# Softmax attention output made turned, with split operands and gates scaled and turned beforehand: one change to a two-layer hybrid decoder kernel

## The chip, the cores and the metric

The kernel runs on one core of one Trainium2 chip. The metric is the device time in microseconds of one execution. Five queues of instructions run side by side on the core and wait for each other by semaphores: TensorE (PE, with its weight loads as PEld), VectorE (DVE), ScalarE (ACT), GpSimd (POOL) and SyncE (SP), which here issues nearly all DMAs.

## The reference

Two layers over 256 positions of 1024 values. In each layer one input projection gives eight groups of 512 columns: query, key, value and gate of four retention heads (rq, rk, rv, rz) and of four softmax attention heads (mq, mk, mv, mz). With 256 positions there is a single block, so the block selection chooses nothing and the softmax attention is plain causal attention with a bias.

```python
for i in range(DEPTH):
    h = rms_norm(x, norm_g[i])
    rq, rk, rv, rz, mq, mk, mv, mz = jnp.split(h @ w_in[i], cuts, axis=-1)
    r_out = retention(rotary(rq), rotary(rk), rv, ret_norm_g[i])   # decayed scores, per-head norm
    r_out = silu(rz) * r_out
    m_out = moba(rms_norm(mq, q_norm_g[i]), rms_norm(mk, k_norm_g[i]), mv, rel_bias)
    m_out = silu(mz) * m_out                                       # softmax(q k + bias) v, gated
    x = x + concatenate([r_out, m_out], -1) @ w_out[i]
    gate = sigmoid(rms_norm(x) @ w_ple_gate[i])
    x = x + gate * rms_norm(p[i] @ w_ple[i], ple_norm_g[i])
```

## The kernel before

**Arithmetic.** Weights and activations are f32. A projection is made of three fast matmuls of 512 columns (lines 405 to 407): each operand is split into a high part, rounded to the fast type f32r, and a low part, the rest, and high x high, high x low and low x high are summed. A split is a cast on ScalarE and a subtraction on VectorE: `Stage.gen` does it for two rows of weights at a time (cast L350, subtraction L353). `three` is the same for an attention product. A few small products (L950, L960, L1010) are plain f32 matmuls instead.

**Layout.** Positions are cut into two halves `m` of 128. A projection's result has positions on the partitions. What must be turned goes through `halves` (a ScalarE copy that parts the 16-bit halves into a tile `u16`, L621), a turning DMA from SP's queue into `w16` (L631), and two VectorE copies per turned tile (L640); `to_parts` then splits it into high and low for a projection, as the tile `yT` (called `a` in the profile).

**Order within a layer.** Input projections in the order mq, mk, rq, rk, mz, mv, rv, rz; after the first ones, at places that `groups` names, the attention products: `moba_scores` (softmax scores, then `probs`: bias, exponential, turning into the tile PT, named PS in the profile); `moba_out` (the softmax product by `pv`, L960, followed at once by the retention scores of the last 128 positions, L1010); `ret_scores` (L932); `ret_out` (the retention product, L960 again). The retention scores are multiplied by the decay on VectorE (`decayed`, L999) before `ret_out` may read them. Then come the output projection (k-rows 4 to 7, the softmax half, first), the embedding product and the gate.

**What sets the order.** TensorE's order is that in which the program is written. The other engines' instructions come from chains (generators) that ask a planner, `Flow`, for an engine, a cost, and what must be there or be free; the planner keeps a clock for each engine and lays the ready instruction with the earliest due time. The planned costs decide only the order: on the chip each engine takes its instructions strictly in that order. `tick` starts a group of products when what it needs is done by the planner's clock, with a margin:

```python
groups.append(([lambda: [PC.get(k) for k in ((0, 0), (1, 0), (1, 2))], both(VC, MV), both(TC, RQ, RK)],
               moba_out, 3, 2.0))
groups.append(([], ret_scores, 2, 2.2))
groups.append(([lambda: [SC.get(h) for h in ("own", 0, 2)], both(VC, RV)], ret_out, 2, 0.3))
```

The last number is the margin in microseconds; the one before is the number of free banks wanted of the four of the accumulator pool `mix`.

**Around the softmax product.** `value` makes V on ScalarE (L868). `gate` makes silu's tanh part, kept in G. `moba_y` takes the product from its bank: for each of four heads one VectorE operation with the reciprocal of the softmax sum and the gate (L978), then `halves` and `to_parts` into `yT`.

## Time and profile before

| what | value |
|---|---|
| median of 3 runs | 296.58 us (296.27 to 297.05) |
| profiled execution: span | 294.1 us |
| profiled execution: own whole time | not on the page; the median lies 2.5 us above the span |
| PE busy | 288.9 us, 98% of the span, 1411 instructions |
| PEld / DVE / ACT / POOL busy | 246.5 / 253.5 / 214.7 / 30.9 us |
| softmax and retention output products (L960), both layers | 96 records, 11.4 us |
| retention and softmax scores in three terms (L932) | 48 records, 6.3 us |

How to read it: the page describes one execution. A plain f32 matmul leaves two records, a fast one leaves one. Matmuls overlap in the pipeline, so the mean duration of a group is longer than the distance between starts; the distance is what a matmul costs in a dense stream, and the same holds on VectorE by some 0.09 us an instruction.

### The profile page before, as it was taken

The page shows a single profiled execution, that of the slowest core. Times are in us where ns is not written, and L with a number is a line of the kernel's source. Part 1 is how long each engine was busy: PE and PEld are TensorE (multiplying, and loading weights), DVE is VectorE, ACT ScalarE, POOL GpSimd, SP SyncE. Part 2 cuts the span into 40 slices and gives each one's busy share as a digit, 9 for nine tenths or more (in the row PEclk, how much of TensorE's full clock was granted, in tenths as well). Part 3 has the DMA queues.
Part 4 walks back from the last instruction along what each step waited for, and adds up shares of the span by engine and source line. Part 5 has one row for each costly group of instructions (what it writes and reads, how often), then busy time and mean ns, then how long its engine had stood idle before and what let it go on. Part 6 is the DMA issues. An engine that isn't in the chain of part 4 may idle for free.

```text
span 294.1 us, 4301 instructions
## 1 busy us (share of the span) xinstructions
PE 288.9 (98%) x1411; PEld 246.5 (84%) x1411; DVE 253.5 (86%) x461; ACT 214.7 (73%) x376; POOL 30.9 (11%) x44
## 2 busy tenths in 40 slices
PE   8999999999999999999999999999999999999994
PEld 4788888888899888888888888888898988888884
DVE  3967799999899999699999589999998797969942
ACT  3979974799747893998585896599646869479411
POOL 5004200000001200022003220000000030001300
PEclk9999999999999999999999999999999999999999
DMA  7999999998969868698689969787999766943021
GB/s 220 378 403 410 290 244 309 377 290 187 245 193 270 337 150 280 152 245 319 166 198 296 370 187 220 281 222 170 242 322 243 274 226 176 295 89 71 0 75 71
DMA packets 61774, 69.77 MB, mean 237 GB/s; under 512 B 46260, under 2 KB 47160, under 8 KB 61624
## 3 DMA queue, kind: packets, MB, share of 16 engines
q1 hardware_dynamic: 61712, 69.50, 79.7%
q8 instruction: 11, 0.18, 0.3%
q14 instruction: 11, 0.09, 0.1%
q0 software_dynamic: 32, 0.01, 0.0%
q10 hardware_dynamic: 8, 0.00, 0.0%
HBM read 57.42 MB, written 1.05 MB: 199 GB/s over the span
## 4 chain that ended last, share of the span: by engine, by line
PE 96%; DMA 2%; SPq 0%; ACT 0%; DVE 0%; issue 0%
PE acc L406 26%; PE acc L405 26%; PE acc L407 26%; PE acc L553 4%; PE mix L960 4%; PE mix L932 2%; DMA a<-in_early 2%; PE mix L407 1%; PE mix L743 1%; PE mix L742 1%; PE mix L406 1%; PE mix L744 1%; PE mix L405 1%; PE mix L1010 1%; PE mix L950 1%; ACT wh L459 0%
## 5 line engine op out<-in xcount | busy, mean ns | idle before, releaser
L405 PE MATMUL acc<-wh,a 128*128 128x512 f32 (+1 forms) x286 | 107.8, 377 | 0.0
L406 PE MATMUL acc<-wl,a 128*128 128x512 f32 (+1 forms) x286 | 107.7, 377 | 0.0
L407 PE MATMUL acc<-wh,a 128*128 128x512 f32 (+1 forms) x286 | 107.4, 376 | 0.0
L353 DVE TENSOR_TENSOR wl<-wst,wh 128x1024 fp32r<-128x1024 f32 x76 | 92.0, 1222 | 9.1 <-ACT wh L350 8.9
L350 ACT CAST wh<-wst 128x1024 fp32r<-128x1024 f32 x76 | 78.6, 1054 | 15.2 <-PE acc L407 6.0
L405 PEld LDWEIGHTS acc<-wh,a 128*128 128x128 f32 x286 | 53.5, 187 | 9.1
L407 PEld LDWEIGHTS acc<-wh,a 128*128 128x128 f32 x286 | 53.5, 187 | 9.0
L406 PEld LDWEIGHTS acc<-wl,a 128*128 128x128 f32 x286 | 53.5, 187 | 8.7
L621 ACT COPY u<-tok 128x1024 uint16<-128x1024 uint16 x30 | 31.1, 1053 | 12.7 <-DVE tok L978 7.9
L657 ACT CAST a<-tmp 128x512 fp32r<-128x512 f32 x20 | 12.4, 618 | 10.9 <-DVE tmp L654 8.3
L621 ACT COPY u<-x_t 128x1024 uint16<-128x1024 uint16 x12 | 12.5, 1042 | 10.2 <-DVE x_t L1138 6.8
L673 POOL TENSOR_TENSOR ro<-rs_t,neghalf 128x4 f32<-128x4 f32 x4 | 5.8, 1460 | 129.0 <-DVE rs_t L671 129.0
L640 DVE COPY tmp<-w 128x512 uint16<-128x512 uint16 x40 | 16.4, 466 | 0.1
L659 DVE TENSOR_TENSOR a<-tmp,a 128x512 fp32r<-128x512 f32 x20 | 13.7, 685 | 0.0
L640 DVE COPY T<-w 128x512 uint16<-128x512 uint16 x32 | 12.9, 467 | 0.7 <-DMA w<-u 0.7
L553 PE MATMUL acc<-wh,a 128*128 128x512 f32 (+1 forms) x42 | 11.3, 387 | 0.3 <-ACT wh L459 0.3
L960 PEld LDWEIGHTS mix<-V,PS 128*128 128x128 f32 x96 | 11.3, 192 | 0.3
L1189 DVE SCALAR_TENSOR_TENSOR tmp<-tmp,E 128x512 f32<-128x512 f32 (+1 forms) x9 | 5.7, 629 | 6.7 <-ACT tmp L1183 3.8
L960 PE MATMUL mix<-V,PS 128*128 128x128 f32 x96 | 11.4, 275 | 0.0
L1186 ACT ACTIVATE tmp<-acc,hr 128x512 f32<-128x512 f32 (+1 forms) x8 | 5.0, 631 | 8.5 <-PE acc L407 8.5
L405 PE MATMUL acc<-T,a 128*128 128x512 f32 (+1 forms) x30 | 11.0, 367 | 0.0
L407 PE MATMUL acc<-T,a 128*128 128x512 f32 (+1 forms) x30 | 10.9, 365 | 0.0
(144 smaller groups left out, 458.2 us busy)
## 6 DMA issues: line engine op xcount, KB each, us to landing
wst<-in_w_in SPq DMA_DIRECT2D x59, 512.0 KB, 6.3
wst<-in_w_out SPq DMA_DIRECT2D x16, 512.0 KB, 6.6
wst<-in_w_gate SPq DMA_DIRECT2D x16, 512.0 KB, 4.6
wst<-in_w_ple SPq DMA_DIRECT2D x4, 512.0 KB, 7.6
wst<-in_early SPq DMA_DIRECT2D x4, 384.0 KB, 7.4
a<-in_early SPq DMA_DIRECT2D x3, 384.0 KB, 5.8
x_t<-in_x SPq DMA_DIRECT2D x1, 1024.0 KB
gb<-in_ple_g SPq DMA_DIRECT2D x2, 512.0 KB, 6.7
```

The source lines that it names most:

```text
L350: nc.scalar.copy(hi, s)
L353: nc.vector.tensor_tensor(lo, s, hi.bitcast(F32), op=ALU.subtract)
L405: nc.tensor.matmul(ps, ah, wh, start=start, stop=False)
L406: nc.tensor.matmul(ps, ah, wl, start=False, stop=False)
L407: nc.tensor.matmul(ps, al, wh, start=False, stop=stop)
L553: nc.tensor.matmul(ps[m][:, sl], (a0.lo if which[0] == "lo" else a0.hi)[:, k, m * P:(m + 1) * P], columns(w, sl), start=start and i + j == ...
L621: nc.scalar.copy(u, src.bitcast(U16).rearrange("p (n t) -> p t n", t=2))
L640: nc.vector.tensor_copy(v, w[:, t].rearrange("p (h b) k -> p h (b k)", h=v.shape[1]))
L657: nc.scalar.copy(h, src)
L659: nc.vector.tensor_tensor(a.lo[:, k0:k0 + 4, m * P:(m + 1) * P], src, h.bitcast(F32), op=ALU.subtract)
L932: nc.tensor.matmul(ps, w[a], x[b], start=i == 0, stop=i == 2)
L960: nc.tensor.matmul(ps[:, h * DH:(h + 1) * DH], lhs(h, m, b), v[:, b, h * DH:(h + 1) * DH], start=b == 0, stop=b == m)
```

## The change

The softmax product is made turned: V is the stationary operand, and the probabilities move, so the product comes out with head dimension on the partitions and positions along the row, as the output projection wants it. For the first block of 128 keys, which all 256 positions see, it is made in three fast rows of 256 columns a head, from split operands; for the second block, which only the last 128 positions see, it stays one plain f32 matmul of 128 columns a head. For this `value` splits the first half of V into high and low (`box["VT"]`), and `probs` splits the first key block of the probabilities, both into places of `yT` that are not yet used. The gate is multiplied by the reciprocal of the softmax sum and turned ahead of the product (`gate_turned`), by `halves`, a turning DMA and copies into PT; `moba_y` then needs one multiplication by the turned gate and the split, two heads at a time, and no turning. The tile for the decayed retention scores, which shares its buffer with PT, is taken in `decayed` and no longer on TensorE's side.

```diff
         def value(g, m, ps):
...
+            if m or g == RV:
+                nc.scalar.activation(V[g][:, m], ps, AF.Copy, scale=scale)
+            else:
+                hi, lo = box["VT"] = [yT.both[:, k].rearrange("p t s -> p (t s)") for k in (6, 7)]
+                nc.scalar.activation(hi, ps, AF.Copy, scale=scale)
+                yield ask(DVE, 0.665)
+                nc.vector.scalar_tensor_tensor(lo, ps, scale, hi.bitcast(F32), op0=ALU.mult, op1=ALU.subtract)
...
             yield from turned(u, lambda: raw[:, :, h0:h0 + per, m * P:m * P + n])
+            src, hi, lo = (v[:, h0:h0 + per, m * P:(m + 1) * P] for v in (box["PT"], yT.hi, yT.lo))
+            yield ask(ACT, 0.1 + 0.11 * per)
+            nc.scalar.copy(hi, src)
+            yield ask(DVE, 0.08 + 0.13 * per)
+            nc.vector.tensor_tensor(lo, src, hi.bitcast(F32), op=ALU.subtract)
...
+        def turn_gates():
+            for m in range(MT):
+                if (MZ, m) in GC and (m, 2 * m) in PC and m not in GTC:
+                    GTC[m] = flow.begin(gate_turned(m), flow.soon(GATES))
+
+        def gate_turned(m):
             ri = small(H, "ri")
-            yield ask(DVE, 0.1)
+            yield ask(DVE, 0.1, after=(GC[MZ, m], *PC.values()))
             nc.vector.reciprocal(ri, DEN[m])
             yield ask(DVE, 0.14)
             nc.vector.tensor_scalar(ri, ri, stats(m)[1], None, op0=ALU.mult)
-            yield ask(DVE, 0.26, take=("tok",), after=(GC[MZ, m],))
...
-                nc.vector.scalar_tensor_tensor(y[:, sl], ps[:, sl], ri[:, h:h + 1], G[MZ][:, m, sl],
-                                               op0=ALU.mult, op1=ALU.mult)
+            yield ask(DVE, 0.605, take=("tok",))
+            o = tok_p.tile([P, GW], F32, name="tok")
+            nc.vector.tensor_tensor(o.rearrange("p (h d) -> p h d", h=H), G[MZ][:, m].rearrange("p (h d) -> p h d", h=H),
+                                    ri[:, :, None].to_broadcast([P, H, DH]), op=ALU.mult)
...
-            u = yield from halves(y, "tok")
-            yield from to_parts(yT, m, 4, u)
+            u = yield from halves(o, "tok")
+            raw = box["PT"].bitcast(U16).rearrange("p h (k t) -> p t h k", t=2)
+            yield from turned(u, lambda: raw[:, :, :, m * P:(m + 1) * P])
+
+        def moba_y(i, ps):
+            yield ask(DVE, 0.605, take=("tmp",), after=tuple(GTC[m] for m in range(MT)))
+            t = tmp_p.tile([P, GW], F32, name="tmp").rearrange("p (h s) -> p h s", h=2)
+            nc.vector.tensor_tensor(t, ps.rearrange("p (h s) -> p h s", h=2), box["PT"][:, i::2, :S], op=ALU.mult)
+            flow.free("mix")
...
+            yield ask(ACT, 0.53)
+            hi, lo = (v[:, H + i::2] for v in (yT.hi, yT.lo))
+            nc.scalar.copy(hi, t)
+            yield ask(DVE, 0.605)
+            nc.vector.tensor_tensor(lo, t, hi.bitcast(F32), op=ALU.subtract)
...
         def moba_out():
-            for m in range(MT):
-                ps = pv(m, lambda h, m, b: box["PT"][:, h, (m + b) * P:(m + b + 1) * P], V[MV])
...
+                for h, d, o in heads:
+                    flow.row(0.342)
+                    three(o, [v[:, d] for v in (vh, vl)], [v[:, h] for v in (yT.hi, yT.lo)], False)
+                for h, d, o in heads:
+                    flow.row(0.22)
+                    nc.tensor.matmul(o[:, P:], V[MV][:, 1, d], box["PT"][:, h, S:], start=False, stop=True)
...
         def decayed(h0, n, cols, ps):
-            yield ask(DVE, 0.605, after=(L_DEC,))
+            own = n == H
+            yield ask(DVE, 0.605, take=("PS",) if own else (), after=(L_DEC,) if own else (L_DEC, SC["own"]))
```

**What the planner makes of it.** Line numbers of helpers move by one (the weight split's subtraction L353 is L354 after, the copies L640 are L641). Names carry buffer numbers here.

TensorE in layer 0, at the softmax product and the own-block scores. Before:

```order
L960 MATMUL mix_971<-V_901,PS_662 128x128 x4
L960 MATMUL mix_980<-V_901,PS_662 128x128 x8
L1010 MATMUL mix_1001<-T_762,T_865 128x128 x4
L405 MATMUL acc_900<-wh_887,a_132 128x512
L406 MATMUL acc_900<-wl_888,a_132 128x512
```

After (L949 is `three`, L1034 the plain matmul of the second key block):

```order
L949 MATMUL mix_1023<-a_139 128x256 x3
L949 MATMUL mix_1024<-a_139 128x256 x3
L1034 MATMUL mix_1023<-PS_662,V_917 128x128
L1034 MATMUL mix_1024<-PS_662,V_917 128x128
L949 MATMUL mix_1023<-a_139 128x256 x3
L949 MATMUL mix_1024<-a_139 128x256 x3
L1034 MATMUL mix_1023<-PS_662,V_917 128x128
L1034 MATMUL mix_1024<-PS_662,V_917 128x128
L1060 MATMUL mix_1048<-T_762,T_867 128x128 x4
```

The product moved behind 18 more projection rows (from the middle of rv's 48 into the first rows of rz); between the own-block scores and `ret_scores` stand twelve rows where six stood, and between `ret_scores` and `ret_out` six where eighteen stood. In layer 1 the product moved behind 30 more rows, with twelve rows in each of the two places.

VectorE in layer 0, from the last copies of probabilities to the softmax product's own operations. Before:

```order
L640 COPY PS_662<-w16_885 128x2x256 x2
L353 TENSOR_TENSOR wl_910<-wst_691,wh_909 128x1024
L767 TENSOR_TENSOR pl_790<-pf_787,ph_789 128x512
L353 TENSOR_TENSOR wl_932<-wst_744,wh_931 128x1024
L640 COPY T_865<-w16_922 128x4x128 x2
L353 TENSOR_TENSOR wl_953<-wst_848,wh_952 128x1024
L969 RECIPROCAL ri_979<-den_663 128x4
L971 TENSOR_SCALAR ri_979<-ri_979,hr_376 128x4
L978 SCALAR_TENSOR_TENSOR tok_987<-mix_971,ri_979,G_810 128x128 x4
L353 TENSOR_TENSOR wl_973<-wst_903,wh_972 128x1024
```

After, the first part (L878 is V's split, L945 the probabilities', L1001 the gate's scaling):

```order
L641 COPY PS_662<-w16_888 128x2x256 x2
L878 SCALAR_TENSOR_TENSOR a_139<-acc_793,rstd_375,a_139 128x512
L945 TENSOR_TENSOR a_139<-PS_662,a_139 128x2x128 x2
L354 TENSOR_TENSOR wl_911<-wst_691,wh_910 128x1024
L996 RECIPROCAL ri_778<-den_663 128x4
L998 TENSOR_SCALAR ri_778<-ri_778,hr_376 128x4
L1001 TENSOR_TENSOR tok_957<-G_812,ri_778 128x512
L996 RECIPROCAL ri_788<-den_664 128x4
L998 TENSOR_SCALAR ri_788<-ri_788,hr_401 128x4
L1001 TENSOR_TENSOR tok_969<-G_812,ri_788 128x512
L814 TENSOR_TENSOR Q2_925<-T_867,Q2_925 128x512
L354 TENSOR_TENSOR wl_938<-wst_744,wh_937 128x1024
```

V's split, two splits of probabilities and the gates' scaling, with its reciprocals, now stand ahead of the product; before, the reciprocals stood behind it.

VectorE in layer 0, where the softmax product's result and the retention decays are taken from their banks (the third part of the same list). Before:

```order
L978 SCALAR_TENSOR_TENSOR tok_1015<-mix_980,ri_999,G_810 128x128 x4
L999 TENSOR_TENSOR PS_1000<-mix_1001,cst_122 128x4x128
L999 TENSOR_TENSOR PS_1000<-mix_1021,cst_122 128x2x256
L999 TENSOR_TENSOR PS_1000<-mix_1033,cst_122 128x2x256
L640 COPY tmp_1051<-w16_1013 128x512 x2
```

After (L1013 is the multiplication by the turned gates, L1021 the split of its result, L1051 the decays):

```order
L354 TENSOR_TENSOR wl_993<-wst_903,wh_992 128x1024
L641 COPY PS_662<-w16_986 128x4x128 x2
L768 TENSOR_TENSOR pl_792<-pf_789,ph_791 128x512
L641 COPY PS_662<-w16_1000 128x4x128 x2
L354 TENSOR_TENSOR wl_1011<-wst_959,wh_1010 128x1024
L1013 TENSOR_TENSOR tmp_1054<-mix_1023,PS_662 128x512
L1013 TENSOR_TENSOR tmp_1060<-mix_1024,PS_662 128x512
L1051 TENSOR_TENSOR PS_1066<-mix_1048,cst_122 128x4x128
L1021 TENSOR_TENSOR a_139<-tmp_1054,a_139 128x2x256
L354 TENSOR_TENSOR wl_1079<-wst_1017,wh_1078 128x1024
L1051 TENSOR_TENSOR PS_1066<-mix_1085,cst_122 128x2x256
L1051 TENSOR_TENSOR PS_1066<-mix_1095,cst_122 128x2x256
```

The copies of the turned gates and one more weight split moved ahead of the operations on the product, and a weight split stands between the own-block decay and the two others. Between the two fences of after stand the copies into T_867 and the weight split wl_962. Six weight splits stand between the first split of keys (L802, L803 after) and the first operation that reads the product, where four stood before.

More of the change, by code (lines that the diff above doesn't have):

```diff
@@ L59 @@
 TURN = 0
+GATES = 6.0
 AHEAD = 1.6
@@ L863, in value @@
         def value(g, m, ps):
-            yield ask(ACT, 0.585, take=() if m else ("V",), after=need_stats(m) + ((VA[g],) if m else ()))
-            if not m:
+            first = m == (g == MV)
+            yield ask(ACT, 0.585, take=("V",) if first else (),
+                      after=need_stats(m) + ((VA[g],) if m and g == RV else ()))
+            scale = stats(m)[0 if g == MV else 2]
+            if first:
                 V[g] = big.tile([P, MT, GW], F32, name="V", bufs=1)
                 flow.reach(VA[g])
-            nc.scalar.activation(V[g][:, m], ps, AF.Copy, scale=stats(m)[0 if g == MV else 2])
+            if m or g == RV:
[5 more added lines that the diff above has]
+                nc.vector.scalar_tensor_tensor(lo, ps, scale, hi.bitcast(F32), op0=ALU.mult, op1=ALU.subtract)
             flow.free("acc")
@@ new lines, in moba_out @@
+        def moba_out():
+            vh, vl = box["VT"]
+            banks = [bank(mix_p, "mix") for _ in range(2)]
+            for h0 in range(0, H, 2):
+                heads = [(h, slice(h * DH, (h + 1) * DH), banks[h - h0][:, h0 * P:h0 * P + S]) for h in range(h0, h0 + 2)]
+                for h, d, o in heads:
[4 more added lines that the diff above has]
+                    nc.tensor.matmul(o[:, P:], V[MV][:, 1, d], box["PT"][:, h, S:], start=False, stop=True)
+            for i, ps in enumerate(banks):
+                c = flow.begin(moba_y(i, ps), flow.soon(3.1))
+                for m in range(MT):
+                    for k in range(H + i, KT, 2):
+                        yT.made[m, k] = c
@@ L1004, in ret_scores_own @@
             q, k = T[RQ], T[RK]
-            flow.take("PS")
-            box["ST"] = big.tile([P, H, S + P], F32, name="PS", bufs=1)
             ps = bank(mix_p, "mix")
@@ L1050, in ret_norm @@
             RO[m] = o
+            flow.reach(RN[m])
         def ret_out():
@@ L1071, in ret_gate @@
             flow.begin(ret_tanh(m, ps, th), flow.soon(1.4))
-            while m not in RC:
-                yield ask(DVE, 0.0)
-            yield ask(DVE, 0.605, take=("tok",), after=(RC[m],))
+            yield ask(DVE, 0.605, take=("tok",), after=(RN[m],))
             y = tok_p.tile([P, GW], F32, name="tok")
```

30 lines of the change are left out of this document (15 added, 15 removed).

## The prediction

> **What bounds the kernel now.** I read the page's busy times first, then TensorE's waits, then the timelines of TensorE (PE) and VectorE (DVE) around the changed product.
>
> ```profile
> span 294.1 us, 4301 instructions
> PE 288.9 (98%) x1411; PEld 246.5 (84%) x1411; DVE 253.5 (86%) x461; ACT 214.7 (73%) x376; POOL 30.9 (11%) x44
> ...
> PEclk9999999999999999999999999999999999999999
> ...
> PE mix L295 <- PEq L1302: 0.8, 1, 0.8
> PE acc L553 <- ACT wh L459: 0.3, 1, 0.3
> ```
>
> TensorE is busy for 98% of the span at an undisturbed granted clock, and its list of waits has two entries, 1.1 us together, both in the first 8 us. So the time is the sum of TensorE's instructions: an instruction saved there is worth its full length, and a new wait there costs its full length, since no later idle time can absorb it. VectorE, at 86%, is the engine to watch.
>
> ```profile
> 78.64 0.38 PE L405 MATMUL acc<-wh,a 128*128 128x512 f32 x1
> ...
> 79.30 2.84 PE L960 MATMUL mix<-V,PS 128*128 128x128 f32 x24
> 81.97 1.06 PE L1010 MATMUL mix<-T 128*128 128x128 f32 x8
> 82.78 0.47 PE L405 MATMUL acc<-wh,a 128*128 128x512 f32 x1
> ...
> 84.20 1.54 PE L932 MATMUL mix<-K,Q 128*128 128x256 f32 x12
> 85.58 0.39 PE L405 MATMUL acc<-wh,a 128*128 128x512 f32 x1
> ...
> 89.57 2.84 PE L960 MATMUL mix<-V,PS 128*128 128x128 f32 x24
> ```
>
> Layer 0, first column the start. Durations overlap in the pipeline, so I use distances between starts. A 512-column row costs 0.22 us (three from 78.64 to 79.30). The softmax product (L960, 12 matmuls in 24 records) takes 2.67 us, 0.22 a matmul. The retention scores of the last 128 positions follow (L1010, 0.9 with the pipeline's change-over), six projection rows, the other retention scores (L932, 12 three-term matmuls of 256 columns) in 1.38, and the retention output product at 89.57.
>
> ```profile
> 71.48 1.30 DVE L802 TENSOR_TENSOR K<-T,K 128x512 fp32r<-128x512 f32 x2
> 72.68 1.23 DVE L353 TENSOR_TENSOR wl<-wst,wh 128x1024 fp32r<-128x1024 f32 x1
> ...
> 76.03 0.82 DVE L640 COPY PS<-w 128x512 uint16<-128x512 uint16 x2 [0.83 <-DMA w<-u]
> 76.74 1.21 DVE L353 TENSOR_TENSOR wl<-wst,wh 128x1024 fp32r<-128x1024 f32 x1
> 77.87 0.68 DVE L767 TENSOR_TENSOR pl<-pf,ph 128x512 fp32r<-128x512 f32 x1
> 78.47 1.22 DVE L353 TENSOR_TENSOR wl<-wst,wh 128x1024 fp32r<-128x1024 f32 x1
> 79.60 0.79 DVE L640 COPY T<-w 128x512 uint16<-128x512 uint16 x2
> 80.29 1.21 DVE L353 TENSOR_TENSOR wl<-wst,wh 128x1024 fp32r<-128x1024 f32 x1
> 81.41 0.17 DVE L969 RECIPROCAL ri<-den 128x4 f32<-128x4 f32 x1
> ...
> 81.96 1.13 DVE L978 SCALAR_TENSOR_TENSOR tok<-mix,ri,G 128x128 f32<-128x128 f32 x4
> ...
> 85.72 1.88 DVE L999 TENSOR_TENSOR PS<-mix,cst 128x512 f32<-128x512 f32 x3
> 87.52 0.82 DVE L640 COPY tmp<-w 128x512 uint16<-128x512 uint16 x2
> ```
>
> VectorE in the same stretch is full except for 0.83 us at 76.03. From starts: a split of two weight rows (L353) 1.13, a 512-column operation 0.60 (L802 twice in 1.20), a pair of copies 0.70, reciprocal and scaling 0.55. One row matters most: the copies into T at 79.60 come after the softmax product has started at 79.30, though `groups` lets the planner place that product only 2.0 us after those copies. At this place VectorE runs at least 3 us later, against TensorE, than the planner's clock believes, and today nothing hangs on it.
>
> **The change, part by part.**
>
> *The product on TensorE.* Before: 12 matmuls, 2.67. After: 12 three-term rows of 256 columns, by L932 1.38, and 4 full-precision matmuls of 128 columns, 4 x 0.22 = 0.89: 2.27. Gain 0.40 a layer, 0.8 in both, all on the path. The Trainium skill, "TensorE: Matmul & The Clock Gate" (Back-to-back issue gap), gives N/2.4 + 2.5 ns, so 109 ns for 256 columns in bf16, where L932 shows 1.38/12 = 115; by the page the gain would be 0.07 larger a layer. I take the row, which is the same form.
>
> *VectorE ahead of the product.* New in each layer: three splits of the probabilities' first key block, one split of V, two gate scalings, and four copies that bring the turned gates home.
>
> ```profile
> L836 DVE TENSOR_TENSOR tok<-acc,qr 128x512 f32<-128x512 f32 x8 | 5.3, 687 | 2.4 <-POOL qr L833 2.4
> L815 DVE SCALAR_TENSOR_TENSOR Q<-T,qkg,Q 128x512 fp32r<-128x512 f32 x2 | 1.5, 741 | 0.0
> L1191 DVE TENSOR_TENSOR x_t<-x_t,tmp 128x256 f32<-128x256 f32 x2 | 0.9, 426 | 0.1
> L657 ACT CAST a<-tmp 128x512 fp32r<-128x512 f32 x20 | 12.4, 618 | 10.9 <-DVE tmp L654 8.3 <-DVE tmp L640 2.5
> w<-u SPq DMA_TRANSPOSE x7, 3.3
> ```
>
> Means are about 0.09 above the distance of starts (687 against 0.60). So the splits are 0.60 + 2 x 0.34 = 1.3 (L1191's small form), the split of V 0.65 (L815), the gates 2 x (0.55 + 0.60) = 2.3 (L836 has their broadcast form), the copies 1.4: 5.65. By VectorE's order in layer 0, six weight splits instead of four also stand between the start of the key splits at 71.48 and the first operation that reads the product: 2.25 more. Before, that point is reached at 81.41; now at 81.41 + 7.9 = 89.3. No form is unknown; bounds come from the two extremes of pace (durations instead of distances for the new instructions, +0.8) and from the 0.83 us of idle time at 76.03 being filled (-0.8): 88.5 to 90.1.
>
> *TensorE comes to the product later too.* In layer 0, 18 more projection rows stand ahead of it: 79.30 + 18 x 0.22 = 83.3, end 85.5. So the multiplication by the turned gates (two instructions in `moba_y`) starts 3.8 us after its operand is there. By itself that harms nothing: its result goes to the output projection, far behind. But VectorE takes its instructions in order, and behind it stand the retention scores' decays, for which TensorE waits next.
>
> *Where TensorE stops.* From 89.3 VectorE has the two multiplications (1.2), the own-block decay (0.6), two splits of the gated result (1.2; ScalarE's two casts, 0.6 each by L657, run beside), one weight split (1.13), two decays (1.2): heads 0 and 1 are ready at 94.1, heads 2 and 3 at 94.7. TensorE from 85.5: own scores 0.9, twelve rows 2.65, scores 1.38, six rows 1.32: it stands at `ret_out` at 91.8. It waits 2.3 for heads 0 and 1, does two matmuls (0.45), waits 0.15 more: 2.45. Before that, the second bank of scores needs a bank that the first multiplication frees at 89.95, when TensorE wants it at 89.8; that shifts, and is not added. I take 2.5, bounds 1.6 to 3.4 with those of 89.3.
>
> *The second layer.*
>
> ```profile
> 212.90 0.85 DVE L640 COPY T<-w 128x512 uint16<-128x512 uint16 x2
> ...
> 215.93 1.25 DVE L353 TENSOR_TENSOR wl<-wst,wh 128x1024 fp32r<-128x1024 f32 x1
> 217.33 1.23 DVE L353 TENSOR_TENSOR wl<-wst,wh 128x1024 fp32r<-128x1024 f32 x1 [0.16 <-ACT wh L350]
> ...
> 217.32 2.84 PE L960 MATMUL mix<-V,PS 128*128 128x128 f32 x24
> ```
>
> Here VectorE is better placed: the copies into T end 3.6 us before the product. The same 5.65 come in, and three more weight splits, 3.4: VectorE reaches the multiplication at 217.33 + 1.13 - 0.27 (the gap before 217.33) + 9.05 = 227.2. The product stands 30 projection rows later, at 217.32 + 6.6 = 223.9, and ends at 226.2: VectorE is 1.0 late. Twelve rows, not six, stand between scores and `ret_out`, so TensorE gets there at 226.2 + 0.9 + 2.65 + 1.38 + 2.65 = 233.8, and VectorE's list (3.0, then a decay that waits for the scores at 230.4, a weight split, a decay) ends at 232.8. Slack 0.9: no wait.
>
> *Costed at nothing.* ScalarE's new casts (about 1.2 a layer) lie beside VectorE's. The number of turning DMAs stays; two a layer move ahead of the product, in SP's queue past two loads of output weights in layer 0 and four in layer 1. They land 3.3 after issue, before VectorE comes to their copies. In layer 1 they also pass the turning of the last retention keys, whose sum on VectorE (L858) moves behind the gates; by the list above its copies end at 225.0, and the own-block scores want them at 226.2. The splits that the product itself reads are done by 78.1 in layer 0, 5 ahead of it. What they push back has cover: the output projection's first row stood at 100.18 in the trace and stands some 4 later now. The chain from product to output projection loses its turning DMA and its copies; nobody waited for it.
>
> *What is late next.*
>
> ```profile
> 89.63 0.69 DVE L659 TENSOR_TENSOR a<-tmp,a 128x512 fp32r<-128x512 f32 x1
> ...
> 92.84 0.69 DVE L1031 BATCH_NORM_STATS2 bst<-mix 128x6 f32<-128x128 f32 x3
> ...
> 109.81 0.68 DVE L659 TENSOR_TENSOR a<-tmp,a 128x512 fp32r<-128x512 f32 x1
> 110.74 0.38 PE L405 MATMUL acc<-K,a 128*128 128x512 f32 x1
> ```
>
> The gated retention rows go from `ret_out` (89.57) to 110.49 in 20.9, and TensorE wants the low half two rows after 110.74. Of VectorE's time in that chain 3.0 (89.63 to 92.84, less one statistic) is the old softmax output's and goes: 17.9. TensorE's way from `ret_out` shortens by 12 rows, 2.65, to about 19. Some 1 us of slack stays, where 0.7 was.
>
> **Sum.** Against the span: 294.1 - 0.8 + 2.5 = 295.8. The page gives no more of the profiled execution than its span; the median of the runs, 296.58, lies 2.5 above, and I keep that: 298.3.
>
> **The rivals.**
>
> *The cover holds, and only the gain shows.* VectorE would have to come to the multiplication 2.45 earlier, before 86.9, in layer 0. For it: the planner set `ret_out` only where its clock had the decays done. Against it: the T copies above show that clock 3 us wrong just here, and the sum of VectorE's rows leaves no gap. Time 296.58 - 0.8 = 295.8, not slower.
>
> *The second layer waits as well.* If VectorE is as late there as in layer 0, 3.8 instead of 1.0, the slack of 0.9 is gone and 1.9 is added: 300.2. For it: my 227.2 rests on a longer sum. Against it: 3.6 us of slack in the row at 212.90.
>
> *The wait lets TensorE's clock fall.*
>
> ```profile
> L295 PE MATMUL mix<-const-bfloat16-1.0 128*128 128x512 bf16 x9 | 4.0, 626 | 0.8 <-PEq L1302 0.8
> ```
>
> The nine warm-up matmuls took 4.0 us, 0.44 each against 0.22 later, so a cold array is half as fast for about that long: if the wait brought this back, 4.0 us of matmuls would cost 2.0 more, 300.3. Against it: 2.45 in two pieces is short, and no row here shows a fall. The Trainium skill (same page, Part 1) puts the fall at an idle window of about 3.4 us; by that rule 2.45 stays below, and the upper bound of 3.4 does not.
>
> **How the numbers follow.** The wait in layer 0 alone: 0.63, with its own range 297.2 to 299.4 (bounds 1.6 to 3.4 less 0.8, and 0.2 for scatter). Cover holds: 0.20, at 295.4 to 296.2. Second layer too: 0.10. Clock: 0.07. 0.3% of this kernel is 0.9 us, about what a measurement can tell from no change. Faster by more is possible only if the cover holds and the gain is a little over 0.8: 0.09. Within it: the rest of that case, 0.11, and the low end of the first, 0.08: 0.19. Slower: 0.72. The range takes in the first case, most of the second and the nearer part of the third: 295.7 to 299.9.
>
> **What would show it.** The product's new rows at about 115 and 220 ns, 2.3 together. On VectorE, the first multiplication by the turned gates about 4 us after the product's end in layer 0 and about 1 in layer 1, with no idle time ahead of it. In TensorE's waits, a new entry of about 2.5 us at the retention output product of layer 0, released by the VectorE decay. I am wrong if that entry is missing, if it stands at another line (the gated retention rows, the own-block scores), or if VectorE idles before the product's end.

## The result, and the profile after

The changed kernel takes 300.35 us (median of six runs, 299.09 to 301.34) against 296.58 for the kernel before (295.90 to 297.46): ratio 1.0116, interval 1.0092 to 1.0141. It is slower by 3.8 us. I had forecast slower by 1.7, at 298.3, with 299.9 as the upper end. The profiled execution took 300.59; its span is 2.1 shorter. The six executions fall into two groups: four have a mean granted clock of 0.991 to 0.994 and take 300.1 to 301.3, two have 0.997 and 1.000 and take 299.1; the kernel before is never below 0.997. Single executions of 1069 us (e1), 1077 us (e3) and 613 us (the kernel before, beside them) lie far from all others, and the times given leave them out.

The page of the changed kernel, busy times and granted clock by slices, then TensorE's list of waits:

```profile
span 298.5 us, 4286 instructions
PE 290.2 (97%) x1403; PEld 247.2 (83%) x1403; DVE 257.9 (86%) x461; ACT 217.0 (73%) x382; POOL 31.2 (10%) x44
...
PEclk9999999999999899999999999999999999999998
```

```profile
PE mix L978 <- ACT T L351: 2.1, 1, 2.1
PE mix L949 <- DVE tmp L1013: 1.3, 1, 1.3
PE mix L296 <- PEq L1351: 0.8, 1, 0.8
PE acc L408 <- DVE her L729: 0.2, 1, 0.2
```

Two new entries of TensorE, 3.4 us together: at the retention output product (L978) and, ahead of it, at the second bank of retention scores (L949). And one digit of the clock is down. The timelines of layer 0, TensorE first (projection rows left out), then VectorE:

```profile
82.40 0.87 PE L949 MATMUL mix<-a 128*128 128x256 f32 x6
...
84.27 0.61 PE L1034 MATMUL mix<-PS,V 128*128 128x128 f32 x4
84.71 1.06 PE L1060 MATMUL mix<-T 128*128 128x128 f32 x8
...
88.27 0.86 PE L949 MATMUL mix<-K,Q 128*128 128x256 f32 x6
90.39 0.96 PE L949 MATMUL mix<-K,Q 128*128 128x256 f32 x6 [1.26 <-DVE tmp L1013]
...
94.80 4.63 PE L978 MATMUL mix<-V,PS 128*128 128x128 f32 x24 [2.10 <-ACT T L351]
99.18 0.47 PE L406 MATMUL acc<-wh,a 128*128 128x512 f32 x1
```

```profile
88.52 1.21 DVE L354 TENSOR_TENSOR wl<-wst,wh 128x1024 fp32r<-128x1024 f32 x1
89.65 1.28 DVE L1013 TENSOR_TENSOR tmp<-mix,PS 128x512 f32<-128x512 f32 x2
91.02 0.69 DVE L1051 TENSOR_TENSOR PS<-mix,cst 128x512 f32<-128x512 f32 x1
91.63 1.28 DVE L1021 TENSOR_TENSOR a<-tmp,a 128x512 fp32r<-128x512 f32 x2
92.83 1.22 DVE L354 TENSOR_TENSOR wl<-wst,wh 128x1024 fp32r<-128x1024 f32 x1
93.97 1.28 DVE L1051 TENSOR_TENSOR PS<-mix,cst 128x512 f32<-128x512 f32 x2
```

The turned product runs from 82.40 to 84.71, 2.31 us. VectorE takes it up (L1013) only at 89.65, 4.9 us later, without a gap in its own rows. Until then no bank is free for the second scores, and the decays (L1051 at 93.97), for which the retention product waits, stand behind the gated result's splits (L1021) and a weight split. The list of waits names a ScalarE cast as the releaser of L978, because that cast ended at 94.77. The decay is the likelier one: the first of the two ended at 94.65, 0.15 ahead of the product, and in e8, g0, f0 and e6 below the distance is the same 0.14 or 0.15, with the decay named. The retention product itself then took 4.38 by starts (94.80 to 99.18), where the same rows took 2.60 before. Windows of 4 us show why (the third number from the end is the granted clock, those ahead of it busy times):

```profile
88.00:92.00 4.00, 2.74 (x18) 2.36 (x18) 3.91 (x7) 1.63 (x3) 0.00 (x0) 1.00 0.94 331
92.00:96.00 4.00, 1.90 (x12) 1.47 (x11) 3.25 (x5) 3.42 (x4) 0.00 (x0) 0.94 1.02 372
96.00:100.00 4.00, 4.00 (x22) 3.90 (x22) 3.07 (x13) 0.65 (x2) 0.99 (x1) 0.63 1.01 415
```

The clock goes 1.00, 0.94, 0.63: behind the idle time TensorE ran slower. Layer 1, TensorE and VectorE:

```profile
231.09 1.06 PE L1060 MATMUL mix<-T 128*128 128x128 f32 x8
...
238.70 2.84 PE L978 MATMUL mix<-V,PS 128*128 128x128 f32 x24
```

```profile
231.90 1.29 DVE L1013 TENSOR_TENSOR tmp<-mix,PS 128x512 f32<-128x512 f32 x2
```

There the product ends at 231.09, where the next rows (L1060) start; VectorE is 0.8 behind, and nothing waits.

### The profile page after: what moved, and what is told of

Its sections match the earlier page's. It is cut to its first block, busy times and chain, and to the rows that moved or that the text cites. A ratio compares the mean times of both kernels' runs of the same rounds, so it can differ in the third digit from the quotient of the medians.

```text
span 298.5 us, 4286 instructions
## 1 busy us (share of the span) xinstructions
PE 290.2 (97%) x1403; PEld 247.2 (83%) x1403; DVE 257.9 (86%) x461; ACT 217.0 (73%) x382; POOL 31.2 (10%) x44
## 3 DMA queue, kind: packets, MB, share of 16 engines
HBM read 57.42 MB, written 1.05 MB: 196 GB/s over the span
## 4 chain that ended last, share of the span: by engine, by line
PE 55%; DVE 6%; ACT 6%; issue 2%; ACTq 0%
PE acc L408 16%; PE acc L406 16%; PE acc L407 16%; DVE wl L354 3%; PE mix L978 2%; PE mix L949 2%; ACT wh L351 2%; ACT u L622 1%; ACT tmp L681 1%; DVE a L660 1%; DVE tmp L641 1%; PE mix L744 1%; PE mix L743 1%; PE mix L745 1%; DVE E L733 0%
## 5 line engine op out<-in xcount | busy, mean ns | idle before, releaser
L406 PE MATMUL acc<-wh,a 128*128 128x512 f32 (+1 forms) x294 | 111.1, 378 | 0.0
L408 PE MATMUL acc<-wh,a 128*128 128x512 f32 (+1 forms) x294 | 110.7, 377 | 0.2 <-DVE her L729 0.2
L407 PE MATMUL acc<-wl,a 128*128 128x512 f32 (+1 forms) x294 | 110.4, 376 | 0.0
L354 DVE TENSOR_TENSOR wl<-wst,wh 128x1024 fp32r<-128x1024 f32 x78 | 94.0, 1219 | 7.7 <-ACT wh L351 7.6
L408 PEld LDWEIGHTS acc<-wh,a 128*128 128x128 f32 x294 | 55.0, 187 | 10.2 <-DVE a L660 0.6
L406 PEld LDWEIGHTS acc<-wh,a 128*128 128x128 f32 x294 | 55.0, 187 | 8.8
L658 ACT CAST a<-tmp 128x512 fp32r<-128x512 f32 x16 | 9.9, 620 | 7.8 <-DVE tmp L655 7.8
L641 DVE COPY T<-w 128x512 uint16<-128x512 uint16 x32 | 13.0, 465 | 0.8 <-DMA w<-u 0.8
L641 DVE COPY tmp<-w 128x512 uint16<-128x512 uint16 x32 | 13.0, 465 | 0.4 <-DMA w<-u 0.3
L660 DVE TENSOR_TENSOR a<-tmp,a 128x512 fp32r<-128x512 f32 x16 | 10.9, 684 | 0.0
L554 PE MATMUL acc<-wh,a 128*128 128x512 f32 (+1 forms) x42 | 10.9, 377 | 0.0
L681 ACT ACTIVATE tmp<-x_t 128x512 f32<-128x512 f32 x16 | 10.0, 623 | 0.5 <-DMA x_t<-in_x 0.5
L978 PE MATMUL mix<-V,PS 128*128 128x128 f32 x48 | 7.5, 327 | 2.1 <-ACT T L351 2.1
L351 ACT CAST T<-wst 128x1024 fp32r<-128x1024 f32 x8 | 8.4, 1049 | 1.5 <-DMA wst<-in_w_in 1.2
L978 PEld LDWEIGHTS mix<-V,PS 128*128 128x128 f32 x48 | 7.3, 238 | 2.6 <-ACT T L351 2.5
```

The lines of the kernel that those rows point to most:

```text
L351: nc.scalar.copy(hi, s)
L354: nc.vector.tensor_tensor(lo, s, hi.bitcast(F32), op=ALU.subtract)
L406: nc.tensor.matmul(ps, ah, wh, start=start, stop=False)
L407: nc.tensor.matmul(ps, ah, wl, start=False, stop=False)
L408: nc.tensor.matmul(ps, al, wh, start=False, stop=stop)
L554: nc.tensor.matmul(ps[m][:, sl], (a0.lo if which[0] == "lo" else a0.hi)[:, k, m * P:(m + 1) * P], columns(w, sl), start=start and i + j == ...
```

## The experiments

Each was timed against the kernel before on the same chip (its median 296.5 to 297.0 each time), with six runs unless said otherwise. My first theory, A: VectorE's list, in its order, is late at one place, TensorE waits behind it, and the idle time lets its clock fall. The rivals grew with the results. TensorE's first projection rows of layer 0 start at 18.00 in the changed kernel's trace and at 18.1 to 18.9 in the others, so a list of waits can also be shorter because TensorE came later.

**Does the idle time make the clock fall? (e3_fill)**

```diff
+            for _ in range(fill):
+                nc.tensor.matmul(ps, ones[:, :P], ones, start=True, stop=True)
```

> In layer 0, ten fast matmuls of 512 columns of constants (10 x 0.22 = 2.2 us) are put ahead of the retention product, into its own bank, where TensorE stood idle for 2.27 us; they change no result and VectorE's list is the same. Theory A with the clock's fall caused by the idle time: TensorE is busy in place of idle, the retention product takes 2.7 us and not 4.4, so 300.3 - 1.7 = 298.6 (the wait itself stays as filling; 298.3 to 299.3). Rival (the fall has nothing to do with that idle time, or the first idle piece of 1.4 us alone starts it): 300.3 with the granted clock again under 0.95 in the 4 us behind.

298.8 us (298.72 to 299.65 in five runs), 1.5 less than the changed kernel and close to the 299.1 of its two executions without the fall. TensorE's timeline:

```profile
92.36 2.36 PE L976 MATMUL mix<-const-bfloat16-1.0 128*128 128x512 bf16 x9
94.61 3.00 PE L980 MATMUL mix<-V,PS 128*128 128x128 f32 x24
97.37 0.48 PE L406 MATMUL acc<-wh,a 128*128 128x512 f32 x1
```

The product starts as late as ever, 94.61, but takes 2.76 in place of 4.38, at clock 1.00, and no execution is below 0.998. The fall is a consequence of the idle time, and costs 1.5 to 1.8 us where it happens. Work that does nothing paid here, and the wait remains.

**Less VectorE work ahead of the wait (e1_no_low_splits, and again for its trace)**

```diff
-                nc.vector.scalar_tensor_tensor(lo, ps, scale, hi.bitcast(F32), op0=ALU.mult, op1=ALU.subtract)
...
-            nc.vector.tensor_tensor(lo, src, hi.bitcast(F32), op=ALU.subtract)
```

> Left out: the low parts of the first key block's probabilities and of V's first half, so VectorE's four subtractions a layer that make them are gone (the product's three-term rows read the high parts three times). TensorE's program stands where it stood. Theory A (VectorE's list in order is late at the product, TensorE waits behind it, and the idle time lets its clock fall): VectorE comes to the multiplication by the turned gates 1.95 us earlier in layer 0 (1.3 for the probabilities, 0.65 for V), TensorE's wait there falls from 3.7 us to about 1.8, the clock does not fall any more: 300.3 - 1.9 - 1.7 = 296.8, bounds 296.0 to 298.5 (the upper end if the clock still falls). Theory B (the wait is set by something else than VectorE's added work, for instance by a turning DMA that lands late): 300.3, no change.

> The same kernel as the first run without the low parts, for its trace. Theory D: VectorE's list is 1.95 us shorter a layer, so of TensorE's waits of 3.7 in layer 0 about 1.8 are left. Theory F: the copies of the turned gates wait for their transfer (landing near 87.9), VectorE idles 1 us or more there, and 2.5 or more of the wait is left.

Of the waits of 3.4 in the list 1.1 is left:

```profile
PE mix L976 <- ACT wh L351: 1.1, 1, 1.1
83.71 0.86 PE L947 MATMUL mix<-a 128*128 128x256 f32 x6
88.48 1.28 DVE L1011 TENSOR_TENSOR tmp<-mix,PS 128x512 f32<-128x512 f32 x2
```

Only about half of that is A's. VectorE came to the multiplication 1.17 earlier (88.48 for 89.65), not 1.95: its rows now hold idle time, 0.90 of it for the transfer of the probabilities. And TensorE reached the product 1.31 later (83.71 for 82.40). The time did not fall with the waits: 299.97 (298.23 to 301.76 in five runs), and 300.56 in the execution with this trace. There TensorE's projection rows stood 0.2267 apart in two stretches, not 0.2200, at a full granted clock; this alone is some 3.7 us (last section). So the time of this kernel says nothing of the wait's price, and I don't use it.

**The product stays, what waits for it comes later (e2_margins)**

```diff
-        groups.append(([], ret_scores, 2, 2.2))
-        groups.append(([lambda: [...], both(VC, RV)], ret_out, 2, 0.3))
+        groups.append(([], ret_scores, 2, 4.2))
+        groups.append(([lambda: [...], both(VC, RV)], ret_out, 2, 4.3))
```

> Only the margins of the retention scores (2.2 to 4.2) and of the retention output product (0.3 to 4.3) are larger: in layer 0 the second scores stand 6 rows later and the retention product 24 rows later than in the changed kernel, so TensorE has 5.3 us more of projection rows ahead of it. Theory A (VectorE late at one place): the wait of 3.7 us at the retention product goes, but VectorE's chain from there to the gated retention rows (about 17.9 us) has only some 15 us of rows beside it, so up to 2.9 us come back as a wait at the output projection: 296 to 298.5. Theory C (TensorE's product is merely placed too early, nothing else is short): 295.8 - 296.2, no wait at all. Theory B (something else than VectorE): 300.3.

304.17 us (1.0257, interval 1.0229 to 1.0285), worse than any case I had. The wait at the retention product is gone and a longer one stands at the rows that read the gated retention output, in both layers:

```profile
PE acc L406 <- DVE tok L1125: 5.5, 3, 2.3
```

The clock fell there too (0.66 between 110 and 115 us), so not all of the loss is wait. There is a second deadline behind the first, and it had no 5 us to give.

**What stands between (e6_late_splits)**

```diff
+    S_IN[0, RZ, 1].late = {c: (DECAYED[0],) for c in range(2)}
+    S_OUT[0, 0, 1].late = {c: (DECAYED[0],) for c in range(2)}
-            yield ask(DVE, 1.135)
+            yield ask(DVE, 1.135, after=self.late.get(c, ()))
```

> Five of VectorE's weight splits of layer 0 that stood ahead of or between the multiplication by the turned gates and the retention decays (of the retention gate's second half and the output projection's first rows) are laid behind the decays; nothing is left out and TensorE's program is the same. Theory A: the three or four of them that stood ahead of the decays (1.13 each) take 3.4 to 4.5 us off VectorE's way to the decays, more than TensorE's waits of 3.7, so the wait is 0.3 or less and the clock stays up: 300.3 - 3.5 - 1.7 = 295.1, plus what comes back at the rows that need the moved splits (0 to 1.5): 295.0 to 297.0. Theory D (VectorE's whole list is the bound, not one place in it): the moved splits are then late themselves and the wait only moves to the rows behind the retention product: 298.5 to 300.3.

The edit names four splits; a fifth stood just behind the decays already. 299.98 us: as rival D said, the wait moved. VectorE's rows, then TensorE's:

```profile
87.91 0.81 DVE L645 COPY PS<-w 128x512 uint16<-128x512 uint16 x2 [1.69 <-DMA w<-u]
...
93.21 5.76 DVE L354 TENSOR_TENSOR wl<-wst,wh 128x1024 fp32r<-128x1024 f32 x5
98.89 0.89 DVE L1087 BATCH_NORM_STATS2 bst<-mix 128x6 f32<-128x128 f32 x4
```

```profile
92.85 3.00 PE L982 MATMUL mix<-V,PS 128*128 128x128 f32 x24 [0.97 <-DVE PS L1055]
...
109.83 0.49 PE L406 MATMUL acc<-wh,a 128*128 128x512 f32 x1 [2.06 <-DVE tok L1131]
```

With the weight splits out of the way VectorE stood 1.69 us for the transfer that turns the gates, which the splits had hidden; and the five splits, laid in one piece, put the statistics of the retention output at 98.89, 2.5 us later than in the changed kernel (96.36) though the product began 1.95 earlier, so the gated rows came 2.06 late.

**Does work taken off anywhere help? (e7, b7, s1, d1)** First three weight splits of layer 0 went to GpSimd, in the changed kernel and in the kernel before:

```diff
-            yield ask(DVE, 1.135)
+            eng, e, us = (POOL, nc.gpsimd, 2.6) if c in self.pool else (DVE, nc.vector, 1.135)
+            yield ask(eng, us)
-            nc.vector.tensor_tensor(lo, s, hi.bitcast(F32), op=ALU.subtract)
+            e.tensor_tensor(lo, s, hi.bitcast(F32), op=ALU.subtract)
```

> Three weight splits of layer 0 (second chunks of the second half of the retention queries, the retention keys and the softmax gate) are subtracted on GpSimd, which stands idle from 34 to 99 us, and not on VectorE; nothing is left out, the order is planned anew. Theory D (VectorE's whole list in layer 0, full from 40 to 117 us, is the bound): 3 x 1.13 = 3.4 us come off it well ahead of the product, TensorE's waits of 3.7 in layer 0 shrink to 0.3 or so and the clock stays up: 300.3 - 3.4 - 1.7 = 295.2, bounds 295.0 to 296.6, so about 0.8 below the kernel before. Theory F (the transfer that turns the gates, landing near 87.9, or the place of the products, is the floor): VectorE idles instead and 298.5 to 300 stay. If GpSimd's subtractions slow VectorE beside them: 297 to 299.

> The kernel before the change with the same three weight splits on GpSimd. Theory D: before, VectorE was full but TensorE did not wait for it, so nothing is gained: 296.6 to 297.0 as before, within 0.3. If VectorE already cost time before (its lists a hidden bound), 295.5 or less.

302.94 and 302.76 us: both 6 us slower, which tells nothing of VectorE's total. The GpSimd group of the first, and a pair of VectorE's copies beside it:

```profile
L355 POOL TENSOR_TENSOR wl<-wst,wh 128x1024 fp32r<-128x1024 f32 x3 | 9.5, 3162 | 13.3 <-DVE K L808 9.7 <-ACT wh L351 3.6
38.33 3.00 DVE L646 COPY T<-w 128x512 uint16<-128x512 uint16 x2
```

3.16 us each in the mean (2.4 to 4.1), where I had planned 2.6 and VectorE takes 1.22. One GpSimd subtraction ran from 37.66 to 40.66, and the pair of copies beside it took 3.00, where the next pair took 0.81: the move also slowed VectorE. The order was planned anew, and TensorE's waits (4.9 us and 6.1 in the two lists, without the one of the start) stand in large part at places that had none. So I took the work off without touching any order: three splits of the softmax value's weights left out of the changed kernel, and the same three done twice in the kernel before.

```diff
+            if c in self.short:                            # s1, changed kernel: three chunks
+                lo = hi
+            else:
+                nc.vector.tensor_tensor(lo, s, hi.bitcast(F32), op=ALU.subtract)
...
+            for _ in range(2 if c in self.twice else 1):   # d1, kernel before: the same three
+                nc.vector.tensor_tensor(lo, s, hi.bitcast(F32), op=ALU.subtract)
```

> The changed kernel with three of layer 0's weight splits left out of VectorE's list (the softmax value's projection: second chunk of its first half, both chunks of its second half; their low rows read the high part), every engine's order otherwise the same. Theory D (VectorE's list in layer 0 is full, so work taken off anywhere ahead comes out at the wait): VectorE reaches the multiplication by the turned gates 3.4 us earlier, TensorE's waits of 3.7 in layer 0 shrink to 0.3 to 0.8, the clock stays up: 300.3 - 3.4 - 1.7 = 295.2, bounds 295.0 to 296.6. Theory F (the turned gates' transfer is the floor): VectorE idles ahead of their copies, and 1.5 us or more of wait is left: 297 to 298.5.

> The kernel before the change with the same three weight splits of layer 0 done twice over on VectorE (the second time writes the same values): 3.4 us more VectorE work, every engine's order otherwise the same, nothing of the change. Theory D: the slack is 0.8 of idle time and 0.7 at the gated retention rows, so TensorE waits 1.9 to 2.7 in layer 0: 298.5 to 299.3, more if the clock falls. If VectorE had room: 296.6.

Left out: 299.57, hardly a gain. VectorE's idle time ahead of 72 us, one of seven such gaps, and the multiplication by the turned gates:

```profile
60.85 0.47 DVE L647 COPY T<-w 128x512 uint16<-128x512 uint16 x1 [1.50 <-DMA w<-u]
...
89.32 1.29 DVE L1019 TENSOR_TENSOR tmp<-mix,PS 128x512 f32<-128x512 f32 x2
```

Of the 3.4 us taken off, 0.3 arrive at the multiplication (89.32 for 89.65). The rest turns into waiting for transfers and for ScalarE between 57 and 69 us. That refutes D in the form in which I wrote it, a list that is full from 40 us on. Done twice in the kernel before: 299.41, 2.7 us slower and just above D's range. VectorE work alone, with nothing of the change, makes seven tenths of its loss. TensorE's waits there:

```profile
69.07 0.50 PE L407 MATMUL acc<-wl,a 128*128 128x512 f32 x1 [0.52 <-DVE wl L354]
83.70 1.13 PE L1014 MATMUL mix<-T 128*128 128x128 f32 x8 [1.32 <-DVE T L644]
109.02 0.50 PE L406 MATMUL acc<-T,a 128*128 128x512 f32 x1 [0.21 <-DVE tok L1080]
114.07 0.49 PE L408 MATMUL acc<-K,a 128*128 128x512 f32 x1 [0.36 <-DVE a L663]
```

VectorE has no room for more, but its pace up to 72 us is also held by transfers and by ScalarE, so less work there buys nothing.

**The copies of the turned gates on ScalarE (e8_gate_copies_act)**

```diff
-            yield ask(DVE, 0.35, take=() if t else take)
+            yield ask(ACT, 0.53) if act else ask(DVE, 0.35, take=() if t else take)
```

> The four copies a layer that bring the turned gates home are made on ScalarE, which stood idle for 4.1 us ahead of its casts of the gated result, and not on VectorE: 1.4 us off VectorE's list just ahead of the multiplication. Theory D: TensorE's waits fall from 3.7 to about 2.3: 300.3 - 1.4 = 298.9, or 297.2 if the clock does not fall any more. If ScalarE's own order makes the copies later than before: 300 or more.

299.78 us (1.0097, interval 1.0066 to 1.0127, which overlaps the changed kernel's). The wait shrank by 1.6: VectorE came to the multiplication 1.25 earlier (88.40) and TensorE to the product 0.6 later (82.98). The fall of the clock stayed in this execution and two others; the three at 0.998 or more took 297.98 to 299.74:

```profile
93.56 4.63 PE L978 MATMUL mix<-V,PS 128*128 128x128 f32 x24 [1.78 <-DVE PS L1051]
```

**Without the fast rows (e5_plain_product, e5c_plain_product)**

```diff
-                    three(o, [v[:, d] for v in (vh, vl)], [v[:, h] for v in (yT.hi, yT.lo)], False)
+                    nc.tensor.matmul(o, V[MV][:, 0, d], box["PT"][:, h, :S], start=True, stop=False)
```

> The turned product is kept, with the gates scaled and turned beforehand, but the first key block is made in one plain f32 matmul of 256 columns a head, from unsplit operands: the splits of V and of the probabilities are gone (VectorE 1.95 us a layer less than the changed kernel), and TensorE's product is as long as before the change (2.67). Theory D (VectorE's total): its list is within 0.2 us a layer of the kernel before, so no wait of more than 1 us is left: 296.6 to 297.6. Theory C (turning the gates beforehand and the products' place are what costs): 299 or more.

In this version the turned gates still go to the tile whose first block the product now reads, so that it read gates and TensorE waited 8.4 us for them: 310.09 us (five runs), which answers nothing of the question. The next keeps them in the gate's own tile:

> The turned product with the gates scaled and turned beforehand, but the first key block is one plain f32 matmul of 256 columns a head from unsplit operands; the splits of V and of the probabilities are gone, and the turned gates stand in the gate's own tile, so that nothing of the product waits for them. TensorE's product is as long as before the change (2.67), VectorE's list within 0.2 us a layer of the kernel before. Theory D: no wait over 1 us is left, 296.6 to 297.6. Theory C (gates ahead and the place of the products are what costs, not VectorE's sum): 299 or more.

299.45 us (1.0103, interval 1.0076 to 1.0130). VectorE has as much to do as in the kernel before, TensorE's product is as long, and 2.8 us are lost all the same, without a fall of the clock (0.997 or more), most of it in three waits:

```profile
PE mix L964 <- DVE PS L1039: 1.1, 1, 1.1
...
PE acc L408 <- DVE a L660: 0.7, 1, 0.7
PE mix L935 <- DVE tmp L1001: 0.5, 1, 0.5
```

So VectorE's sum alone does not set the loss; where the work or the products stand does, and this run does not part the two. On VectorE, what had been done behind the decays, where the old output's copies and splits stood, now stands ahead of them.

**The decays first (g0, f0, f4)** If the place counts, the decays should come before whatever does not have to precede them: the gated result's splits (g0); the same with the gate copies on ScalarE (f0); and one weight split of the output projection behind them too (f4).

```diff
-            yield ask(DVE, 0.605)
+            yield ask(DVE, 0.605, after=() if l else (DECAYED[0],))     # L1021's splits
+    S_OUT[0, 0, 1].late = {c: (DECAYED[0],) for c in (1,)}              # f4 only
```

> Only the order: in layer 0 the two retention decays stand ahead of the two splits of the gated result on VectorE. Theory A: 1.2 us less VectorE work ahead of the decays, wait 3.7 - 1.2 = 2.5 in two pieces; the clock may still fall: 297.9 to 299.1. Theory D: 300.3, the wait moved.

> In layer 0 the two retention decays stand ahead of the two splits of the gated result on VectorE, and the copies of the turned gates are on ScalarE; nothing else. Theory A (what counts is the VectorE work between the probabilities' transfer at 76 us and the decays): 2.6 us less of it than in the changed kernel, so of 3.7 some 0.7 to 1.1 of wait are left at the retention product, no fall of the clock, and no new wait at the gated retention rows (VectorE 0.3 late where 0.8 was spare): 296.6 - 0.8 + 0.9 = 296.7, bounds 295.9 to 297.7. Theory D (the sum of VectorE's work up to the gated retention rows): the sum is the same as with the copies on ScalarE alone, and the wait reappears at the output projection: 298.5 to 299.8.

> As the first of these, and one weight split of the output projection (second chunk of its first stage) also laid behind the decays. Theory A for the retention product: no wait there. But VectorE then reaches the statistics of the retention output 2 to 3 us late, and the gated retention rows have 0.8 to spare: a wait of 1 to 2 us at the output projection: 297 to 298.5. If that chain has more room: 295.8.

g0 took 299.51, 0.4 above A's upper end, and its three executions at clock 0.997 or more (298.06 to 298.95) lie inside; but the first decay ended only 0.46 earlier than in the changed kernel (94.19 for 94.65). f0 took 300.45, far from A's numbers, and 299.15 and 299.53 even where the clock stayed up. VectorE's rows in f0:

```profile
90.90 0.69 DVE L1053 TENSOR_TENSOR PS<-mix,cst 128x512 f32<-128x512 f32 x1
92.61 1.23 DVE L354 TENSOR_TENSOR wl<-wst,wh 128x1024 fp32r<-128x1024 f32 x1 [1.02 <-ACT wh L351]
93.75 1.28 DVE L1053 TENSOR_TENSOR PS<-mix,cst 128x512 f32<-128x512 f32 x2
```

With the splits gone, the weight split that also stands ahead of the decays reached its turn before its cast on ScalarE was done, and VectorE waited 1.02 us in front of decays that were ready (0.86 in g0). f4 moves that weight split as well: 298.54 (1.0065, interval 1.0039 to 1.0091), the shortest time of the change with nothing left out. No wait at the retention product, the clock at 0.997 or more in all six executions, and, as expected, a wait at the output projection:

```profile
PE acc L406 <- ACT a L661: 0.9, 1, 0.9
...
PE mix L952 <- DVE tmp L1016: 0.6, 1, 0.6
PE acc L408 <- DVE a L663: 0.4, 1, 0.4
PE acc L406 <- DVE tok L1130: 0.3, 1, 0.3
```

**Both deadlines (h1_f4_no_low_splits)** f4's order, and e1's four subtractions a layer left out.

> As the kernel with the decays first, the gate copies on ScalarE and one weight split late, and the four subtractions a layer for the low parts of the probabilities and of V left out (the product reads the high parts three times). Theory G (two deadlines, the retention product and the gated retention rows, and VectorE full from 76 us to the second: order decides only at which of them TensorE waits, VectorE's net work there how long): the waits of 2.9 us in layer 0 shrink by 1.95 to about 1.0, 298.5 - 1.9 = 296.6, bounds 296.0 to 297.4. Rival (the transfers of the turned gates or ScalarE set the pace): VectorE idles instead, 297.8 or more.

296.95 us (296.62 to 297.41 in twelve runs), ratio to the kernel before 1.0012, interval 1.0001 to 1.0022. Of the waits two are left, at the gated rows:

```profile
PE acc L406 <- ACT a L661: 0.8, 1, 0.8
...
PE acc L408 <- DVE a L663: 0.4, 1, 0.4
```

Theory G gave 296.6, bounds 296.0 to 297.4, and the rival 297.8 or more. The time is G's, in part by luck: of the 1.6 us between f4 and h1, 1.05 lie in the span (medians 296.05 and 295.0); the rest is the distance from span to time, 2.5 in f4 and 1.9 in h1, for which no run shows a cause. In the list the waits went from 2.2 to 1.2, some half of what G said for 1.95 us of work; TensorE's first rows start alike (18.83 and 18.84). What the runs support is this: between the transfer of the probabilities at about 76 us and the gated retention rows at about 112, VectorE hardly stands idle (busy for 33.9 of these 36 us in h1) and there are two deadlines. Order decides at which of them TensorE waits, and less work on VectorE shortens the wait. That VectorE alone sets the pace is not shown: the wait of 0.8 that is left is put down to a ScalarE cast.

No version that computes everything beat the kernel before. One that needs 1.95 us less of VectorE's work and leaves nothing out, e5c's plain product, I did not run in f4's order. Its product took 2.79 for 2.31 in layer 0; with that twice on top of h1's 296.95 I estimate 297.9 for it.

## Why the prediction was off

The step that failed is the clock: the sum put its fall at nothing, and it cost 1.79 us of the 2.7 by which the span missed. The wait was mis-sized as well, 3.8 for 2.5, but 0.9 of that is only TensorE's earlier start. A short wait in the gate section (0.42), put at nothing too, and the product (0.08) make up the rest. The place of the wait and the engine behind it were right.

*The product on TensorE.* Right: 2.31 us for the forecast 2.27. The gain is 0.36 a layer by starts.

*VectorE ahead of the product, layer 0.* Right. The multiplication was forecast for 89.3 and stood at 89.65, with no gap ahead of it in VectorE's rows, as the sum needed.

*TensorE's arrival.* I carried over the position from the trace of before: product at 83.3, end 85.5. It ended at 84.71, because the first projection rows of layer 0 started 0.91 earlier in this execution (18.00 for 18.91). VectorE did not share that, so what TensorE gained at the start it lost again at the first wait.

*The wait.* 2.5 us forecast, 3.8 found (from starts, less what the same rows take without a wait: 1.54 at the second scores and 2.26 at the retention product; 3.4 in the list, which takes the pipeline's tail off). I wrote that the bank wait "shifts, and is not added". As a sum it is right that the first gap delays arrival at the second, but the whole was fixed by when the decays end, 95.2 for my 94.7, and by when TensorE would have arrived, 91.0 for my 91.8. Those two together are the 1.3 that were missing. The place, the releasing engine's list and the order of the gaps were as described.

*The clock.* The failing step. I gave the fall a chance of 0.07, and it happened: 1.79 us on the retention product, in four of six executions. The reason I gave against it, "2.45 in two pieces is short", was wrong by measurement (e3_fill). That this rival's own figure, 300.3, is almost the measured 300.35 is partly luck: its wait was 1.3 too short, and the earlier start took 0.9 off. The two executions without the fall, at 299.1, lie inside my range. The Trainium skill, "TensorE: Matmul & The Clock Gate" (Part 1), gives an idle window of about 3.4 us, and I let that keep the chance low; here the clock fell after gaps of 1.26 and 2.10 us, and in e8 after a single one of 1.78. The measurement decides.

*The second layer.* Right: VectorE 0.8 late for the forecast 1.0, no wait.

*From span to time.* I added 2.5, the distance of the median from the profiled span. In the runs of both kernels for which I have both numbers, time minus span is 1.9 to 2.1 (of the experiments up to 2.6), so some 0.5 of this term was the profiled execution of before being faster than its median. Against the profiled execution of the changed kernel it hid that much of the miss.

*The account in the span, by starts:* 294.1, product -0.72, waits in layer 0 +3.80, slower retention product +1.79, a short wait in the gate section at 139 us with what follows it +0.42, earlier start -0.91: 298.5, as measured.

*Costed at nothing.* The turning transfer of the gates landed in time only because weight splits stood in front of its copies (1.69 us of idle time in e6). ScalarE's cover was also thinner than I wrote: 1.02 and 0.86 us of VectorE's idle time in f0 and g0. And "some 1 us of slack" at the gated rows was right in size: every order that cleared the first deadline ran into it.

## What to carry to other kernels

When one engine is busy 98% and another stands next to it, count the second engine's work between two points where data must be there (here a transfer's landing and a product), not its share of the span: that count predicted the place of the wait and the engine behind it. Then give the wait a price above its length, since TensorE's clock may fall behind it (here 1.5 to 1.8 us, in four of six executions), and take the engines' positions from more than one execution, because a microsecond of offset between them is a microsecond of wait. Before moving work ahead of a product, look at what stands behind it in the same queue.

## What the runs showed of the hardware

The granted clock fell after gaps much shorter than I had thought, but not after each. In the changed kernel's trace it was 0.50 from 96 to 98 us, 0.52 to 99, then 1.00 again, and the retention product's records started 0.21 us apart for 0.11. Retention product (2.6 at full clock), with the gaps ahead of it in the list: after the change 1.26 and 2.10, 4.38 us; e8 a single one of 1.78, 4.39; g0 0.28 and 1.84, 4.30; s1 0.84 and 2.10, 3.91; f0 0.49 and 2.02, 2.76; e6 0.97, 2.76. A gap of 2.06 ahead of projection rows in e6 left the clock at 1.00, and so did one of 2.82 at the second scores in b7. Even one program does both: the changed kernel four times out of six (0.991 to 0.994), f0 four times, g0, e8 and e6 three times each. Length alone does not decide it, and what does is open. So the changed kernel has two times, 299.1 and some 300.6, and its median depends on how often the clock fell.

In one execution (e1's trace) TensorE's 512-column rows ran at another rhythm in whole stretches, changing only at attention products, with the clock at 1.00: the 138 rows from 18.43 to 49.71 took 31.28 us, where the same 138 rows took 30.36 in the trace of the changed kernel. The window shows 138 rows in 31 us:

```profile
18.00:49.00 31.00, 31.00 (x138) 25.81 (x137) 25.48 (x46) 26.55 (x62) 5.30 (x6) 1.00 1.03 311
```

I have no cause for it. It is a reason to read a wait's price from the waits and the starts, and not from one kernel's total.
